# Byte offsets for split weights and gathered tokens, and 256-column gate/up matmuls in half of the experts

## The chip, the cores and the metric

One core of one Trainium2 chip. The metric is the device time of one execution in microseconds (us), the median of the runs shown. The inputs are fixed, so the tokens are routed in the same way in every run.

## The reference

Three transformer layers over 256 tokens of width 1024, in float32. Layer one mixes by bidirectional gated linear attention and windowed attention and has a dense SwiGLU of width 2816. Layers two and three mix by compressed attention and a gated recurrence; the second has a dense SwiGLU, the third a mixture of 8 experts of width 3584, of which each token takes two. The part that the change is about:

```python
logits = jnp.einsum('td,de->te', xf, w_router)
top_logits, top_idx = lax.top_k(logits, TOP_K)
gates = jax.nn.softmax(top_logits, axis=-1)
...
hid = jax.nn.silu(lax.ragged_dot(xs, w_gate, group_sizes)) * lax.ragged_dot(xs, w_up, group_sizes)
ys = lax.ragged_dot(hid, w_down, group_sizes)
```

## The kernel before

**Split weights.** Each product of float32 operands is made of three matmuls in the type `float32r`: both operands are split into a rounded part `hi` and a rest `lo`, and hi·hi, lo·hi and hi·lo are added up in PSUM. A weight arrives by SP's DMA as a `raw` tile of 128 partitions and up to 2048 floats (`load`, L148). `part_of` splits it in parts of 1024 floats: ScalarE copies it to `hi` (L160), VectorE subtracts (L161). The `hi` and `lo` tiles of a part come from a pool `hip` with three buffers of each, used in turn; until the mixture of experts begins, a fourth place in the turn is the pool `hip2` with one of each.

**Dense part (0 to about 930 us).** Most projections go through `feat`, whose matmuls are issued by the helper `mm` (L196): the weight's 128 columns are stationary, and 256 tokens move (256 columns). A part of 512 output features is 24 such matmuls, 16 with `hi` and 8 with `lo`. `ffn` issues its down projection through `mm` as well. Some projections go through `tok_part` (L225, L226, L228), with tokens stationary and 512 columns of the weight moving.

**Mixture of experts (about 945 us to the end).** `dispatch` gathers the tokens of a pair of experts into `xs` (hi and lo, 128 slots for each expert) by matmuls with one-hot maps (L1293). `expert` walks over 7 blocks of 512 hidden features. `up` computes gate and up: `xs` is stationary, 512 columns of the weight move, six matmuls to a part (L1371, L1372, L1374). `down` does the down projection (L1411, L1413, L1415), also with 512 moving columns; `turned` transposes the hidden block for it (L1392). An explicit order (`Steps`, under a manual schedule) lets the splitting run two parts ahead of the matmuls. Weights arrive in 14 `raw` buffers, used in the order `RAW_ORDER`; nine of them (`raw2`) lie over memory that the dense part's tiles give back, and the order of the list is that in which these bytes come free.

**Where the tiles lie.** In the program's allocation the start addresses in a partition, modulo 128 bytes, are:

| tile | bytes modulo 128 |
|---|---|
| `hi`, `lo` in `hip` (three of each) | 64 |
| `hi`, `lo` in `hip2` | 0 |
| dense activations `nh`, `nl`, `oh`, `ol`, attention's `hh`, `hl` and so on (pool `t4p`, 4096 bytes each) | 0 |
| gathered tokens `xs` (both) | 32 |
| hidden activations `th`, `tl` | 96 |
| dispatch: one-hot maps `oh` (moving), tokens `hh`, `hl` (stationary) | 32, 64 |

Steps of k and of columns inside these tiles are multiples of 512 bytes, so the table holds for every full-width matmul on them.

Of the kernel before, what the change touches and what calls it, by code (L numbers as in the profile page):

```python
# [10 lines left out]
F32 = mybir.dt.float32  # L11
# [8 lines left out]
P = 128  # L20
T = 256
NT = 2
# [11 lines left out]
# weight parts by which pieces of the arithmetic are put off, so that their operands are ready  # L34
# [4 lines left out]
RAW_BUFS, RAW2_BUFS, HI_BUFS, T4_BUFS, OHT_BUFS = 4, 9, 3, 16, 2  # L39

# [72 lines left out]
def tile_kernel(ctx: ExitStack, tc: tile.TileContext, a: dict, out: bass.AP, dbg=None, upto=99):  # L113
# [10 lines left out]
    hip = ctx.enter_context(tc.tile_pool(name="hip", bufs=HI_BUFS))  # L124
# [10 lines left out]
    hi_pools = [hip] * HI_BUFS  # L135
# [3 lines left out]
    # ---------------------------------------------------------------- weights  # L139
    def load(src, k0, kt, c, n, pieces=None):  # L140
        """Rows of k tiles k0.. and columns c.. of a weight; pieces: (column, width) in order."""
# [11 lines left out]
    def part_of(raw, k0, j, m, n):  # L153
        """k tiles j to j + m - 1 of a loaded weight, split in two."""
        pool = hi_pools[hi_turn[0] % len(hi_pools)]
        hi_turn[0] += 1
        hi = pool.tile([P, 1024], F32R, tag="hi", name="hi")[:, :m * n]
        rj = raw[:, j * n:(j + m) * n]
        lo = pool.tile([P, 1024], F32R, tag="lo", name="lo")[:, :m * n]
        nc.scalar.copy(hi, rj)  # L160
        lo_engine[0].tensor_sub(lo, rj, hi.bitcast(F32))  # L161
        return k0 + j, m, hi.rearrange("p (k n) -> p k n", n=n), lo.rearrange("p (k n) -> p k n", n=n)
# [3 lines left out]
    def unit(src, k0, kt, c, n, pieces=None):  # L166
        """A loaded weight's parts."""
# [9 lines left out]
    def defer(n, f):  # L177
        """f() after n more weight parts, and after what was deferred before."""
        queue.append((max([ticks[0] + n] + [d for d, _ in queue]), f))

    def run():
        """What is due."""
        while queue and queue[0][0] <= ticks[0]:
            queue.pop(0)[1]()
# [5 lines left out]
    def tick():  # L190
        """A weight part is done with."""
        ticks[0] += 1
        run()
# [4 lines left out]
    def feat(ps, x, src, c, widths, K, step=4, in_turn=False):  # L198
        """ps[:w, f, :] = src[:, c + f..].T @ x for feature blocks f (weights stationary); in_turn: block
        by block, so that the first are done early."""  # L200
# [18 lines left out]
    def tok_part(o, x, t, part, first, last, cs=slice(None)):  # L219
        """o += x.T @ part for one token tile."""  # L220
# [16 lines left out]
    # ---------------------------------------------------------------- small helpers  # L237
    def rsqrt_of(v, n, y=None):
        """v ** -0.5 on [P, n]."""
# [5 lines left out]
    def rsqrt(ss, n, dim):  # L245
        """(ss / dim + eps) ** -0.5 on [P, n]."""
# [9 lines left out]
    # ---- columns of vectors: gains of the norms ahead of the dense layers  # L256
# [31 lines left out]
    def squares(j, t):  # L288
        """Sum of squares over D of the half j of x, tokens on partitions."""
# [3 lines left out]
    def rstd(dst):  # L293
        """The factor of x's norm, tokens on partitions, from the sums of squares."""
# [6 lines left out]
    with ExitStack() as dense:  # L301
# [21 lines left out]
        class HL:  # L323
            """k-tiled operand kept in several tiles of four k each."""
# [8 lines left out]
        class Norm:  # L333
            """x times the gains n, feature-major and split; what is left of the norm is a factor per token:
            rt [P, t] with tokens on partitions, rb [P, T] along the free axis."""
# [10 lines left out]
            def block(self, k):  # L346
                """Feature block k of x is final."""
# [5 lines left out]
            def squares(self, j):  # L353
                """Blocks 4 j to 4 j + 3 are final."""
# [18 lines left out]
        def bcast_free(dst, cols_):  # L373
            """dst [P, T] = the token-major columns [P, t] along the free axis, on every partition."""
# [7 lines left out]
        def residual(ps, j, nt):  # L382
            """x's feature blocks 4 j to 4 j + 3 take ps [P, 4, T]; the norm nt takes them on."""
# [7 lines left out]
        def ffn(nt, w_gate, w_up, cg, cu, w_down, nxt):  # L391
            """x += (silu(h @ w_gate) * (h @ w_up)) @ w_down."""
# [4 lines left out]
            def down(b):  # L397
                f0, w, hh, hl = b
                for u0 in range(0, w // P, 2):
# [3 lines left out]
                    # feature block by feature block at the end, so that the first are done early  # L403
# [38 lines left out]
        # ============================================================ block 1  # L442
        with ExitStack() as b1:
# [37 lines left out]
            # columns of vectors: gate biases, rope gains  # L481
# [30 lines left out]
            # ---- GLA gates  # L512
# [25 lines left out]
            # ---- SWA projections  # L538
# [16 lines left out]
            def rope(z, nh, n):  # L555
                """z [P, nh, T] feature-major, in place."""
# [18 lines left out]
            for d in range(2):  # L575
# [5 lines left out]
                # factor across the two blocks: exp(r0 - tot0 - r1)  # L581
# [24 lines left out]
            # A[s, t] per head  # L606
# [3 lines left out]
            def scores(b):  # L610
# [5 lines left out]
                # block b of s against the other block of t: forward from 0 to 1, backward from 1 to 0  # L616
# [7 lines left out]
            # ---- SWA attention, by groups of four heads that share keys and values  # L624
# [102 lines left out]
            # ---- silu(r) * gain  # L727
# [10 lines left out]
            # ---- GLA output  # L738
# [37 lines left out]
            # ---- gates and the two output projections  # L776
            def gated(base, j, src, w):
                """sigmoid(h @ w_in[base..]) * (src @ w) for feature blocks 4 j to 4 j + 3."""
# [34 lines left out]
        # ============================================================ block 2  # L813
        b2p = dense.enter_context(tc.tile_pool(name="b2p", bufs=1))
        b2r = dense.enter_context(tc.tile_pool(name="b2r", bufs=1))
        # x itself is a buffer too until its tokens come back to the partitions
# [13 lines left out]
        # ---- rotary tables of the positions, [feature, token]  # L830
# [25 lines left out]
        # ---- columns of vectors  # L856
# [8 lines left out]
        # the second layer's lower bounds, from the cumulative softmax over the layers less its first row, and  # L865
        # what they leave of 1; the first layer's are that row less itself
# [21 lines left out]
        def hsplit(hi, lo, src, ncols_k, gcol):  # L888
            """hi + lo = src * gain, per k tile (gain varies over partitions and k)."""
# [6 lines left out]
        def layer_mix(l, nt, nxt):  # L896
            w_in = a["w_in_2"][l]
            hT, rt_, rb = nt.xT, nt.rt, nt.rb
            # ---- HGRN2: forget gates, keys (feature-major)
# [13 lines left out]
            # log of max(f, 1e-30) in two ranges, as Ln holds down to 2 ** -64  # L913
# [10 lines left out]
            # ---- HGRN2 queries  # L924
# [7 lines left out]
            # ---- HGRN2 attention matrix, from decays between tokens by binary splits  # L932
# [4 lines left out]
            def put(m, h, lhs, rhs):  # L937
                """A[s, t] for the pairs of level m: t in the right halves of 2 h tokens (all tokens if h is 0)."""
# [43 lines left out]
            # ---- MLA: compressed projections  # L982
# [16 lines left out]
            # rstd of both, token-major  # L999
# [23 lines left out]
            # k_pe, rotated, on both halves of the partitions  # L1023
# [12 lines left out]
            # queries  # L1036
# [26 lines left out]
            # keys and values  # L1063
# [23 lines left out]
            # ---- MLA attention  # L1087
# [44 lines left out]
            # ---- chunks of 64: from the chunk's start, and to its end  # L1132
# [29 lines left out]
            # ---- HGRN2 values, silu(g) * gain  # L1162
# [12 lines left out]
            # ---- HGRN2 output  # L1175
# [32 lines left out]
            for j in range(2):  # L1208
# [6 lines left out]
                # x, and the router's logits, short of the norm's factor  # L1215
                for i in range(4):
# [7 lines left out]
                    if k % 2:  # L1224
                        # x with tokens on partitions, and split for the dispatch
# [25 lines left out]
    # ================================================================ mixture of experts  # L1251
    with ExitStack() as moe:
# [6 lines left out]
        # in the order in which their bytes are left  # L1259
# [16 lines left out]
        def dispatch(base, pos_of, gate_of, n):  # L1276
            """One-hot maps and split inputs of n experts, for ranks base..base + 127, step by step."""
# [6 lines left out]
            xs = [m2.tile([P, KD, n * P], F32R, tag="xs%d" % i, name="xs", bufs=1) for i in range(2)]  # L1284
# [18 lines left out]
            # slot-major: who sits where, with which gate and factor  # L1303
# [370 lines left out]
```

## Time and profile before

| | |
|---|---|
| median of 3 runs | 1959.42 us (1956.49 to 1961.25) |
| profiled execution, first to last instruction (span) | 1958.2 us |
| TensorE (PE) busy | 1920.8 us, 98% |
| TensorE weight load (PEld) busy | 1686.8 us, 86% |
| VectorE (DVE) busy | 1534.9 us, 78% |
| ScalarE (ACT) busy | 1262.5 us, 64% |
| read from HBM | 501.20 MB, 256 GB/s over the span |

The profile gives no time of the profiled execution other than its span; the span is 1.2 us below the median, and inside the scatter of the runs. A matmul's record has a start that is measured and an end that is modelled, and records overlap; how fast matmuls follow each other is read from the starts, as the length of a stretch divided by the matmuls that start in it. A count in a row for a stretch contains those that began before it and are still under way. PEclk is the granted TensorE clock as a share of 2.4 GHz.

### The profile page before, as it was taken

Reading aid. Unit: us, or ns where it says so; the run is one execution under the profiler, and the core shown is the slowest. Engines: PE = TensorE matmul, PEld = TensorE weight load, DVE = VectorE, ACT = ScalarE, POOL = GpSimd, SP = SyncE. Lnnn points to the kernel's source line nnn. Section 1 sums busy time; section 2 is a strip of 40 time slices with the busy share of each in tenths; the row PEclk is TensorE's granted clock in tenths of the full one; section 3 lists DMA queues with packets and bytes.
Section 4 is the critical chain, followed back from the end, with each engine's and each line's share of the span. In section 5 each row is a group of like instructions: output and inputs, shape, how many; then the busy total and the mean of one; then the engine's idle time right before and its main releaser. Section 6 shows DMA issues by size and latency. Waiting matters only on the chain.

```text
span 1958.2 us, 29578 instructions
## 1 busy us (share of the span) xinstructions
PE 1920.8 (98%) x11581; PEld 1686.8 (86%) x11581; DVE 1534.9 (78%) x1648; ACT 1262.5 (64%) x1528; POOL 114.3 (6%) x111
## 2 busy tenths in 40 slices
PE   8999999999999999999899999999999999999997
PEld 7879999999989999988788888888888888888886
DVE  5865577557767555875788999889899898988997
ACT  5565455445665444655677777777777777777775
POOL 0110000000210000022000000000000000000000
PEclk9999999999999999999899999999999999999999
DMA  7435555554435555425899998999989999899990
GB/s 284 163 104 183 196 190 184 195 184 144 148 129 172 195 184 169 159 90 178 314 364 353 362 356 319 368 363 351 366 316 357 357 360 365 314 365 362 352 348 34
DMA packets 229458, 504.23 MB, mean 257 GB/s; under 512 B 12500, under 2 KB 25632, under 8 KB 229312
## 3 DMA queue, kind: packets, MB, share of 16 engines
q1 hardware_dynamic: 229312, 502.28, 72.0%
q8 instruction: 92, 1.51, 0.3%
q14 instruction: 54, 0.44, 0.1%
HBM read 501.20 MB, written 1.05 MB: 256 GB/s over the span
## 4 chain that ended last, share of the span: by engine, by line
PE 53%; DVE 1%; ACT 0%; POOL 0%; issue 0%; DVEq 0%; POOLq 0%; ACTq 0%
PE gu L1371 11%; PE gu L1372 11%; PE gu L1374 11%; PE pd L1411 5%; PE pd L1413 5%; PE pd L1415 5%; PE tp L1392 1%; PE tp L1293 1%; PE accum L196 1%; PE tp L1465 0%; PE tp L1466 0%; PE pa L1220 0%; PE tp L1307 0%; DVE hn L1613 0%; PE pd L1424 0%; PE pd L1428 0%
## 5 line engine op out<-in xcount | busy, mean ns | idle before, releaser
L161 DVE TENSOR_TENSOR lo<-raw,hi 128x1024 fp32r<-128x1024 f32 x937 | 1114.7, 1226 | 249.2 <-ACT hi L160 237.0
L160 ACT CAST hi<-raw 128x1024 fp32r<-128x1024 f32 x939 | 954.9, 1042 | 413.6 <-PE accum L196 213.9
L1371 PE MATMUL gu<-hi,xs 128*128 128x512 f32 x896 | 356.1, 397 | 0.0
L1372 PE MATMUL gu<-hi,xs 128*128 128x512 f32 x896 | 355.7, 397 | 0.0
L196 PE MATMUL accum<-nh,hi 128*128 128x256 f32 (+1 forms) x1192 | 288.0, 282 | 0.9 <-DVE hq L929 0.8
L196 PE MATMUL accum<-nl,hi 128*128 128x256 f32 (+1 forms) x1192 | 287.2, 281 | 0.4 <-DVE nl L351 0.4
L1374 PE MATMUL gu<-lo,xs 128*128 128x512 f32 x896 | 282.7, 397 | 0.0
L196 PEld LDWEIGHTS accum<-nh,hi 128*128 128x128 f32 (+1 forms) x1192 | 227.0, 190 | 2.2 <-ACT hi L160 0.9
L196 PEld LDWEIGHTS accum<-nl,hi 128*128 128x128 f32 (+1 forms) x1192 | 226.7, 190 | 1.1 <-DVE nl L351 0.7
L1374 PEld LDWEIGHTS gu<-lo,xs 128*128 128x128 f32 x896 | 168.9, 189 | 41.3
L1371 PEld LDWEIGHTS gu<-hi,xs 128*128 128x128 f32 x896 | 169.1, 189 | 40.7
L1372 PEld LDWEIGHTS gu<-hi,xs 128*128 128x128 f32 x896 | 169.0, 189 | 40.8
L196 PE MATMUL accum<-nh,lo 128*128 128x256 f32 (+1 forms) x1192 | 166.6, 281 | 2.4 <-DVE lo L161 2.4
L196 PEld LDWEIGHTS accum<-nh,lo 128*128 128x128 f32 (+1 forms) x1192 | 150.7, 190 | 3.5 <-DVE lo L161 2.8
L1411 PE MATMUL pd<-hi,th 128*128 128x512 f32 x440 | 143.0, 406 | 0.0
L1413 PE MATMUL pd<-hi,tl 128*128 128x512 f32 x440 | 138.4, 396 | 0.0
L1415 PE MATMUL pd<-lo,th 128*128 128x512 f32 x440 | 138.1, 395 | 0.0
L1415 PEld LDWEIGHTS pd<-lo,th 128*128 128x128 f32 x440 | 82.7, 188 | 20.2
L1413 PEld LDWEIGHTS pd<-hi,tl 128*128 128x128 f32 x440 | 82.6, 188 | 20.2
L196 PE MATMUL pa<-hh,lo 128*128 128x256 f32 x352 | 97.7, 278 | 0.0
L196 PE MATMUL pa<-hl,hi 128*128 128x256 f32 x352 | 97.7, 278 | 0.0
L196 PE MATMUL pa<-hh,hi 128*128 128x256 f32 x352 | 97.7, 278 | 0.0
(439 smaller groups left out, 2362.0 us busy)
## 6 DMA issues: line engine op xcount, KB each, us to landing
raw<-in_moe_w_gate_dram SPq DMA_DIRECT2D x112, 1024.0 KB
raw<-in_moe_w_up_dram SPq DMA_DIRECT2D x112, 1024.0 KB
raw<-in_moe_w_down_dram SPq DMA_DIRECT2D x112, 1024.0 KB
raw<-in_w_in_dram SPq DMA_DIRECT2D x40, 1024.0 KB
raw<-in_w_ffn_in_dram SPq DMA_DIRECT2D x22, 1024.0 KB
raw<-in_w_ffn_out_dram SPq DMA_DIRECT2D x11, 1024.0 KB
raw<-in_w_out_dram SPq DMA_DIRECT2D x10, 1024.0 KB
raw<-in_dense_w_up_dram SPq DMA_DIRECT2D x10, 1024.0 KB
```

What stands on the lines that cost most here:

```text
L160: nc.scalar.copy(hi, rj)
L161: lo_engine[0].tensor_sub(lo, rj, hi.bitcast(F32))
L196: nc.tensor.matmul(o, w, v, start=start, stop=stop, skip_group_check=True)
L1293: nc.tensor.matmul(px[:, kk, :n * P], src[:, t, (k + kk) * P:(k + kk + 1) * P], oh[:, t].rearrange("p n s -> p (n s)"), start=i == 0, stop ...
L1371: nc.tensor.matmul(st[key], xh[:, k, ss], hi[:, k - k0, :], start=k == 0, stop=False)
L1372: nc.tensor.matmul(st[key], xl[:, k, ss], hi[:, k - k0, :], start=False, stop=False)
L1374: nc.tensor.matmul(st[key], xh[:, k, ss], lo[:, k - k0, :], start=False, stop=k == KD - 1)
L1392: nc.tensor.transpose(pt[:, k * P:(k + 1) * P], hd[:, k * P:(k + 1) * P], ident)
L1411: nc.tensor.matmul(pd[z], th[:, ks], hi[:, 0, halves[z]], start=k == 0, stop=False)
L1413: nc.tensor.matmul(pd[z], tl[:, ks], hi[:, 0, halves[z]], start=False, stop=False)
L1415: nc.tensor.matmul(pd[z], th[:, ks], lo[:, 0, halves[z]], start=False, stop=k == 4 * nb - 1)
```

## The change

- `hip` becomes three pools of one buffer for each of `hi` and `lo`, with tiles of 1056 floats in place of 1024, and so do `hip2`'s. Within its tile a part's `hi` starts at the first and its `lo` at the second number of `SKEW` (in floats of 4 bytes). The turn through the pools is now counted from the start of the kernel, modulo the pools there are (four, later three).
- `xs` is allocated with 32 floats more, and its two tiles start at the offsets of `XSKEW`, one pair of offsets for each pair of experts.
- In experts 4 to 7, gate and up use two matmuls of 256 columns (the two halves of the PSUM bank) for each one of 512, with the same stationary operand. All gate/up matmuls are now issued through `mm`.
- Comments are deleted, and a tile `mm` is renamed `mx2`.

```diff
+SKEW = ((0, 4), (8, 12), (2, 20), (8, 12))
+XSKEW = ((0, 4), (8, 12), (16, 20), (24, 28))
+NARROW = (False, False, True, True)
+SPARE = 32
...
-    hip = ctx.enter_context(tc.tile_pool(name="hip", bufs=HI_BUFS))
+    hips = [ctx.enter_context(tc.tile_pool(name="hip%d" % n, bufs=1)) for n in range(HI_BUFS)]
...
-    hi_pools = [hip] * HI_BUFS
+    hi_pools = list(hips)
...
         pool = hi_pools[hi_turn[0] % len(hi_pools)]
+        at = SKEW[hi_turn[0] % len(hi_pools)]
         hi_turn[0] += 1
-        hi = pool.tile([P, 1024], F32R, tag="hi", name="hi")[:, :m * n]
+        hi = pool.tile([P, 1024 + SPARE], F32R, tag="hi", name="hi")[:, at[0]:at[0] + m * n]
         rj = raw[:, j * n:(j + m) * n]
-        lo = pool.tile([P, 1024], F32R, tag="lo", name="lo")[:, :m * n]
+        lo = pool.tile([P, 1024 + SPARE], F32R, tag="lo", name="lo")[:, at[1]:at[1] + m * n]
...
-            xs = [m2.tile([P, KD, n * P], F32R, tag="xs%d" % i, name="xs", bufs=1) for i in range(2)]
+            xs = []
+            for i in range(2):
+                z = m2.tile([P, KD * 2 * P + SPARE], F32R, tag="xs%d" % i, name="xs", bufs=1)
+                o = XSKEW[turn][i]
+                xs.append(z[:, o:o + KD * n * P].rearrange("p (k s) -> p k s", s=n * P))
...
+                    cols = [slice(0, 256), slice(256, 512)] if narrow else [slice(0, 512)]
                     for k in range(k0, k0 + m):
-                        nc.tensor.matmul(st[key], xh[:, k, ss], hi[:, k - k0, :], start=k == 0, stop=False)
-                        nc.tensor.matmul(st[key], xl[:, k, ss], hi[:, k - k0, :], start=False, stop=False)
+                        for z, w in ((xh, hi), (xl, hi)):
+                            for cs in cols:
+                                mm(st[key][:, cs], z[:, k, ss], w[:, k - k0, cs],
+                                   z is xh and k == 0 and cs.start == 0, False)
                     for k in range(k0, k0 + m):
-                        nc.tensor.matmul(st[key], xh[:, k, ss], lo[:, k - k0, :], start=False, stop=k == KD - 1)
+                        for cs in cols:
+                            mm(st[key][:, cs], xh[:, k, ss], lo[:, k - k0, cs], False, k == KD - 1)
...
-                              wg[e], wu[e], wd[e], hold)
+                              wg[e], wu[e], wd[e], hold, NARROW[e // 2])
```

The new tiles are 4224 bytes, 33 times 128, so every pool's start keeps its place modulo 128 bytes; tiles behind them move up by 768 or 1024 bytes. The start addresses after the change, modulo 128: `hi` and `lo` are at 64 and 80, at 96 and 112, at 72 and 16 in the three pools, and at 32 and 48 in `hip2`; `xs` (hi and lo) is at 32 and 48 for experts 0 and 1, at 64 and 80 for 2 and 3, at 96 and 112 for 4 and 5, at 0 and 16 for 6 and 7.

## Rows read from the trace of the kernel before

**Rows 1.** The page: busy time, and the chain that ended last by line

```profile
PE 1920.8 (98%) x11581; PEld 1686.8 (86%) x11581; DVE 1534.9 (78%) x1648; ACT 1262.5 (64%) x1528; POOL 114.3 (6%) x111
PE gu L1371 11%; PE gu L1372 11%; PE gu L1374 11%; PE pd L1411 5%; PE pd L1413 5%; PE pd L1415 5%; PE tp L1392 1%; PE tp L1293 1%; PE accum L196 1%; PE tp L1465 0%; PE tp L1466 0%; PE pa L1220 0%; PE tp L1307 0%; DVE hn L1613 0%; PE pd L1424 0%; PE pd L1428 0%
```

**Rows 2.** Stretches of 100 us: busy time by engine (instructions), clock, DMA share, GB/s

```profile
core 0: us, PE busy (x) PEld busy (x) DVE busy (x) ACT busy (x) POOL busy (x), PEclk, DMA share, GB/s
200.00:300.00 100.00, 99.42 (x860) 98.96 (x859) 67.06 (x65) 49.35 (x53) 3.94 (x2) 1.00 0.55 189
700.00:800.00 100.00, 100.00 (x872) 100.00 (x871) 62.90 (x59) 48.09 (x53) 6.36 (x3) 1.00 0.51 167
1200.00:1300.00 100.00, 100.00 (x442) 80.66 (x441) 90.50 (x87) 76.34 (x82) 0.00 (x0) 1.00 0.97 356
1500.00:1600.00 100.00, 100.00 (x442) 80.67 (x441) 90.15 (x86) 76.03 (x82) 0.00 (x0) 1.00 0.98 359
```

**Rows 3.** Stretches of L196's matmuls, one part of 24 each

```profile
215.77:218.49 2.72, 2.72 (x27) 2.72 (x26) 1.00 0.60 190
218.49:221.37 2.88, 2.88 (x27) 2.88 (x26) 1.00 0.52 198
221.37:224.09 2.72, 2.72 (x27) 2.72 (x26) 1.00 0.94 332
...
226.81:229.53 2.72, 2.72 (x27) 2.72 (x26) 1.00 0.55 160
229.53:232.41 2.88, 2.88 (x27) 2.88 (x26) 1.00 0.69 228
...
596.58:599.41 2.83, 2.83 (x27) 2.83 (x25) 1.00 0.00 0
```

**Rows 4.** Stretches of 512-column matmuls: six, six and 36 start in them

```profile
155.12:156.48 1.36, 1.36 (x8) 1.13 (x7) 0.61 (x1) 0.30 (x1) 0.00 (x0) 1.00 0.00 0
156.48:157.88 1.40, 1.40 (x8) 1.12 (x7) 0.62 (x1) 0.75 (x1) 0.00 (x0) 1.00 0.47 118
1066.41:1074.84 8.43, 8.43 (x37) 6.78 (x36) 7.00 (x7) 6.67 (x8) 0.00 (x0) 1.00 1.00 359
```

**Rows 5.** The chain in order of time, 1188 us: dispatch's 256-column matmuls

```profile
1188.52 0.95 PE tp L1293 x8
```

**Rows 6.** Groups of instructions by line and shape: count, busy us, mean ns

```profile
L1371 PE MATMUL gu<-hi,xs 128*128 128x512 f32 x896 | 356.1, 397 | 0.0
L196 PE MATMUL accum<-nh,hi 128*128 128x256 f32 x1176 | 284.3, 282 | 0.9 <-DVE hq L929 0.8 <-ACT nh L350 0.2
L196 PE MATMUL pa<-hh,hi 128*128 128x256 f32 x352 | 97.7, 278 | 0.0
L196 PE MATMUL accum<-oh,hi 128*128 128x256 f32 x128 | 33.3, 284 | 0.0
L196 PE MATMUL accum<-gol,hi 128*128 128x256 f32 x64 | 15.1, 278 | 0.0
L1411 PE MATMUL pd<-hi,th 128*128 128x512 f32 x440 | 143.0, 406 | 0.0
```

**Rows 7.** The splits at L161 from 1000 to 1900 us: duration ns min/median/max

```profile
L161 DVE TENSOR_TENSOR lo<-raw,hi x606: 1207/1219/1227, 999.5 to 1899.8; 128x1024 fp32r<-128x1024 f32 x152
```

**Rows 8.** In order of time around the experts' start: SP, ACT, POOL and PE

```profile
896.33 0.37 SPq L148 DMA_DIRECT2D raw<-in_moe_w_gate_dram  x1
931.41 3.39 SPq L148 DMA_DIRECT2D raw<-in_moe_w_up_dram  x2
919.42 2.00 ACT L160 CAST hi<-raw 128x1024 fp32r<-128x1024 f32 x2 [1.68 <-PE accum L196]
921.50 2.95 POOL L161 TENSOR_TENSOR lo<-raw,hi 128x1024 fp32r<-128x1024 f32 x1 [11.49 <-ACT hi L160]
954.65 2.93 ACT L160 CAST hi<-raw 128x1024 fp32r<-128x1024 f32 x3
944.07 0.63 PE L1371 MATMUL gu<-hi,xs 128*128 128x512 f32 x1
```

More of the change, by code (lines that the diff above doesn't have):

```diff
@@ L1274, in bc, with dispatch @@
             return z[:, :, None].to_broadcast([P, NT, NE])
-        def dispatch(base, pos_of, gate_of, n):
+        def dispatch(base, pos_of, gate_of, n, turn=0):
             oh = m2.tile([P, NT, n, P], F32R, tag="oh", name="oh", bufs=1)
@@ L1356, in run, with expert @@
                     self.now += 1
-        def expert(steps, xs, ss, ohT, gs, wg, wu, wd, hold=None):
+        def expert(steps, xs, ss, ohT, gs, wg, wu, wd, hold=None, narrow=False):
             nb = EXPERT_FF // 512
@@ L1491, in pair @@
         def pair(e0):
-            return dispatch(0, lambda t, j: pos[:, t, e0 + j:e0 + j + 1], lambda t, j: gr[:, t, e0 + j, :], 2)
+            return dispatch(0, lambda t, j: pos[:, t, e0 + j:e0 + j + 1], lambda t, j: gr[:, t, e0 + j, :], 2, e0 // 2)
         def dispatched(gen, box, steps):
@@ L1567, in tile_kernel @@
             nc.vector.tensor_scalar(one[n], place, float(n), None, op0=ALU.is_equal)
-        mm = mp.tile([P, 2, NT], F32, name="mm")
+        mx2 = mp.tile([P, 2, NT], F32, name="mx2")
         gp = mp.tile([P, 2, NT], F32, name="gp")
-        nc.vector.reduce_max(mm[:, 0, :], lg, axis=AX.X)
+        nc.vector.reduce_max(mx2[:, 0, :], lg, axis=AX.X)
         nc.vector.scalar_tensor_tensor(place, one[0], -3e38, lg, op0=ALU.mult, op1=ALU.add)
-        nc.vector.reduce_max(mm[:, 1, :], place, axis=AX.X)
-        nc.vector.tensor_sub(gp[:, 1, :], mm[:, 1, :], mm[:, 0, :])
+        nc.vector.reduce_max(mx2[:, 1, :], place, axis=AX.X)
+        nc.vector.tensor_sub(gp[:, 1, :], mx2[:, 1, :], mx2[:, 0, :])
         nc.vector.tensor_mul(gp[:, 1, :], gp[:, 1, :], rr)
```

## The prediction

> **What bounds the kernel now.** I read the page first, then stretches of 100 us, then the stretches of single parts. TensorE is busy for 98% of the span, and its gate, up and down matmuls hold half of the chain that ended last [rows 1]. The stretches show two regimes: 860 to 872 matmuls in 100 us in the dense part and 442 among the experts, with TensorE busy all of both, at the full clock of 2.4 GHz; among the experts DVE is busy for 90% and the DMA engines for 97% [rows 2]. So in most of the span the end is set by how closely matmuls follow each other, and the change can only act through that, or by making something else late.
>
> A matmul of 256 columns streams for 256/2.4 = 106.7 ns. In the dense part 24 of them take 2.72 us or 2.88 us, 113.3 or 120.0 ns each [rows 3]. The pattern repeats with every fourth part: three at the low level, one at the high. The turn has four places, and by the table of addresses three of these hold the weight 64 bytes off the tokens (modulo 128), the fourth, `hip2`, 0 bytes off. I take it that the fourth place is the slow one, since its address is what sets it apart. A stretch near 597 us has the good placement and still takes 2.83 us, 117.9 ns [rows 3], so the address is not all. The 512-column matmuls, 213.3 ns of streaming, take 226.7 or 233.3 ns with the weight 64 bytes off, and 36 in 8.43 us, 234.2 ns, among the experts, where it is 32 off [rows 4]. Two matmuls of 256 columns at the low level take 226.7 ns and at the high level 240.0, so one pair lies on either side of one wide matmul.
>
> **The dense part.** By the counts of a third of its 256-column matmuls [rows 6] there are 3 x (1176 + 352 + 128 + 64 + 64 + 64) = 5544, the two groups of 64 not shown being of the same kind, or 58 sets of four parts of 24. A set costs 72 x 113.3 + 24 x 120.0 = 11.04 us now. Afterwards only the 16 matmuls with the first pool's `hi` keep their place against the tokens. The other 80 lie 16 to 112 bytes off, in no case 0, and at none of these does the trace show a dense matmul. Bounds: all at the low level saves 24 x 6.7 x 58 = 9.3 us; all 80 at the high level costs 56 x 6.7 x 58 = 21.7 us. I take the middle, 116.7 ns, which is near the only 256-column row with another offset (dispatch's one-hot maps against tokens, 32 bytes off: eight in 0.95 us, 118.8 ns each [rows 5]): 16 x 113.3 + 80 x 116.7 = 11.15 us a set, **+6.4 us**.
>
> **Experts 4 to 7, gate and up.** Half of 3 x 896 = 2688 wide matmuls [rows 6] become 1344 pairs. The low level gives 7.5 ns back a pair, -10.1 us; the high level costs 5.8, +7.8 us. For experts 4 and 5 the offsets between weights and `xs` are 0, 16, 24 bytes and the like, and I take dispatch's 118.8 ns, from the same stage: 672 x (237.5 - 234.2) = +2.2 us. For experts 6 and 7 the first pool's `hi` is 64 bytes off the high half of `xs`, as in the good dense row; I take the middle, 233.4 ns a pair, -0.5 us. Together **+1.7 us**. Every half needs its own weight load; the dense part shows loads keeping up with matmuls 113.3 ns apart (PEld busy 100% [rows 2]), so the load is no new bound below that.
>
> **Experts 0 to 3, and the down projection.** 1344 wide matmuls of gate and up and 3 x 440 + 24 of down [rows 6] get new offsets. Wide matmuls 64 and 32 bytes off differ by about 1 ns [rows 4], so I take **0**. Bounds: all at the shortest, 226.7 ns, -20 us; all at twice the high level, +15 us. The DMA engines cap a gain: at 97% busy [rows 2] they leave about 3% of 1000 us, 30 us.
>
> **What costs nothing.** The renamed tile and the comments do nothing. DVE's split takes 1207 to 1227 ns whatever buffers it reads [rows 7]; were it slowed by an 8-byte start, its 10% of idle time among the experts would cover a tenth. Single-buffer pools rotate as the three did, except once: the first expert part takes the place of the last dense part instead of the next one. Its cast, now the second of the two at 919.42, must then wait for TensorE's last dense matmul near 931; the cast of 1 us and POOL's 2.95 us end by 935, and the first expert matmul is at 944.07 [rows 8]. Queued behind that cast on ACT are the copies of x for dispatch, which have the same cover.
>
> The larger tiles also move the dense activations up by 1024 bytes and the `raw2` buffers laid over them by 768, so that a `raw2` buffer reaches 256 bytes into one more dense tile. The fifth expert load, issued on SP at 896.33, then needs the tile that holds `ol` until the last dense matmuls, and SP's queue, which is in order, would hold it and all loads behind it until 931, where the thirteenth is issued now [rows 8]. ACT first wants the fifth in the last of the three casts from 954.65 [rows 8]; 1 MB at 356 GB/s [rows 2] takes 2.9 us. Cover: 20 us. **0**.
>
> **Sum.** 6.4 + 1.7 = +8.1 us on the span of 1958.2; the median of the runs is 1.2 us above the span, so 1967.5 us, 0.4% slower. A difference of 0.3%, 5.9 us, is about what a measurement can tell from none.
>
> **The rivals.** *The offsets end the stalls.* It is on the other side. If only 0 bytes off is bad, the dense part loses its fourth slow part (-9.3 us), and pairs at the low level save up to 10.1 us: 1940 us. For it: the one slow place is the one with 0 bytes off [rows 3]. Against: dispatch's 118.8 ns at 32 bytes off [rows 5], and 117.9 ns at 64 [rows 3]. It decides from a dense mean below 115.0 ns, the mean of 3 x 113.3 and 120.0. Chance 0.20.
>
> *The place is nothing.* If the fourth place is slow for another reason than its address, the dense part stays as it is and a pair takes twice the dense mean, 230.0 ns: 1344 x -4.2 = -5.6 us, 1954 us. Against it: nothing but the address sets the fourth place apart, and a reason tied to the place in the turn would have to spare the next three. Chance 0.25. The Trainium skill, "SBUF — State Buffer", section "Who interferes with whom", gives TensorE two independent read ports, for the moving operand and for the weight load, and says that it never waits on anyone; by that rule the place could do nothing. The trace does not bear it out: the same matmul takes 113.3 or 120.0 ns by its buffer [rows 3]. Its page "TensorE: Matmul & The Clock Gate", section "Wait — 56ns, not 53.3ns?", speaks against the narrow pairs: a stream of matmuls pays some 2.5 ns a matmul above its columns, by which 1344 more would cost an estimated 3.4 us; the trace's 6.7 and 20.9 ns above the columns [rows 3, 4] are not one such price.
>
> *The experts start late.* If the held loads or the cast cost more than their cover, TensorE stands still near 944; ten us past the cover gives 1977. Against it are 9 and 20 us of cover [rows 8]. Chance 0.05.
>
> **Chances and range.** The forecast has 0.50. Of it 0.10 lies within 0.3% (dense nearer the low level). The place being nothing sits on the edge of 0.3%, so 0.06 of its 0.25 counts as faster. Faster 0.20 + 0.06 = 0.26, same 0.10 + 0.19 = 0.29, slower 0.40 + 0.05 = 0.45. The range goes from 1944 (half of the first rival is below) to 1984 (the dense part's upper bound is 1959.4 + 21.7 = 1981, and the pairs add to it). The forecast's own range is 1961 to 1981.
>
> **What would show it.** Parts of 24 in the dense part: the first place mostly at 2.72 us, the others at 2.8 us instead of 2.72, and the fourth below 2.88. Pairs among experts 4 and 5 near 237 ns, and lower in 6 and 7; wide matmuls of experts 0 to 3 still near 234. The first expert matmul within 1 us of where it is now, measured from the last dense one. I am wrong if the fourth place alone changes, if wide matmuls move by more than 2 ns, or if TensorE idles near 944.

## The result, and the profile after

| | before | after |
|---|---|---|
| median, in one job | 1957.95 us | 1970.77 us (1969.29 to 1971.33) |
| span of the profiled execution | 1958.2 us | 1967.4 us |
| last matmul of the dense part starts | 930.88 us | 941.98 us (+11.10) |
| first expert matmul starts | 944.07 us | 955.49 us (+11.42) |
| from there to the end | 1014.11 us | 1011.91 us (-2.20) |

The kernel became slower: the ratio is 1.0061, with an interval of 1.0048 to 1.0075. One disturbed execution of 3842.47 us is left out. The forecast of 1967.5 us was right in sign and 3.3 us low, but the table shows that the sum was not put together as forecast: the dense part lost more than the whole, and the experts gave some of it back.

The page of the changed kernel, busy time and the chain by line, answers to [rows 1]. L202 is `mm`, L196 before; gate and up are now issued there too, which is why their three lines of before are one.

```profile
PE 1931.0 (98%) x12925; PEld 1764.6 (90%) x12925; DVE 1536.9 (78%) x1648; ACT 1262.7 (64%) x1528; POOL 115.6 (6%) x111
PE gu L202 32%; PE pd L1425 5%; PE pd L1427 5%; PE pd L1429 5%; PE tp L1406 1%; PE tp L1303 1%; PE accum L202 1%; PE tp L1479 0%; PE tp L1480 0%; PE tp L1317 0%; DVE hn L1627 0%; DVE ranks L1535 0%; PE pd L1438 0%; PE pd L1439 0%; PE pd L14
```

TensorE has 1344 matmuls more and is still busy for 98%; VectorE and ScalarE are as busy as they were. What bounds the kernel has not changed. The same stretches of 100 us as in [rows 2], for the changed kernel:

```profile
core 0: us, PE busy (x) PEld busy (x) DVE busy (x) ACT busy (x) POOL busy (x), PEclk, DMA share, GB/s
200.00:300.00 100.00, 99.52 (x839) 99.09 (x838) 64.69 (x65) 48.44 (x53) 1.95 (x2) 1.00 0.55 188
700.00:800.00 100.00, 100.00 (x846) 100.00 (x845) 56.28 (x51) 43.32 (x45) 6.33 (x3) 1.00 0.53 171
1200.00:1300.00 100.00, 100.00 (x450) 81.53 (x449) 91.33 (x89) 77.24 (x84) 0.00 (x0) 1.00 0.96 348
1500.00:1600.00 100.00, 100.00 (x714) 93.66 (x713) 89.28 (x85) 76.66 (x83) 0.00 (x0) 1.00 0.99 357
```

Busy time says nothing here: TensorE is 100% busy in both kernels, at the same granted clock. Read the counts. In the dense part 872 matmuls in 100 us became 846, so each takes longer; among experts 2 and 3 (1200 us) 442 became 450, so each takes less. The stretch at 1500 us has two narrow matmuls in place of each wide one of gate and up and can't be compared by its count.

Parts of 24 matmuls in the dense part, at L202 of the changed kernel (compare [rows 3]; start to start of a part, and its length):

```profile
212.95:215.79 2.84, 2.84 (x27) 2.84 (x25) 1.00 0.07 25
215.79:218.62 2.83, 2.83 (x27) 2.83 (x25) 1.00 0.62 201
218.62:221.46 2.84, 2.84 (x27) 2.84 (x25) 1.00 0.49 185
221.46:224.29 2.83, 2.83 (x26) 2.83 (x25) 1.00 0.88 334
```

The pattern of three parts at 2.72 us and one at 2.88 is gone. All four places take 2.83 or 2.84 us, 118.1 ns a matmul. Among the experts, parts of six 512-column matmuls of gate and up (experts 0 and 1), and of twelve 256-column ones (experts 4 and 5), both of the changed kernel:

```profile
1060.06:1061.46 1.40, 1.40 (x8) 1.14 (x6) 1.00 1.04 402
1061.46:1062.84 1.38, 1.38 (x7) 1.13 (x6) 1.00 1.06 405
1062.84:1064.23 1.39, 1.39 (x7) 1.12 (x6) 1.00 1.07 396
...
1643.72:1645.14 1.42, 1.42 (x12) 1.42 (x12) 1.00 1.06 405
1645.14:1646.56 1.42, 1.42 (x15) 1.42 (x14) 1.00 0.81 251
```

A wide part was 8.43/6 = 1.405 us before [rows 4] and is about 1.39 now; a part that became narrow takes 1.42. And the start of the experts, TensorE in order of time, changed kernel:

```profile
941.86 0.40 PE L202 MATMUL accum<-oh,lo 128*128 128x256 f32 x2
942.77 0.61 PE L1226 MATMUL pa<-wr,xT 128*128 128x8 f32 x4 [0.51 <-DVE xT L1224]
...
949.73 0.35 PE L1564 MATMUL tp<-sel,ranks 128*128 128x8 f32 x1 [3.84 <-DVE one L1581]
...
955.49 0.89 PE L202 MATMUL gu<-hi,xs 128*128 128x512 f32 x3
```

What TensorE waits for here is the routing on VectorE, in both kernels (3.70 us before, 3.84 now at the longest). No weight and no cast is late.

### The profile page after: what moved, and what is told of

It reads as the page before. It is cut to its first block, busy times and chain, and to the rows that moved or that the text cites. A ratio compares the mean times of both kernels' runs of the same rounds, so it can differ in the third digit from the quotient of the medians.

```text
span 1967.4 us, 32281 instructions
## 1 busy us (share of the span) xinstructions
PE 1931.0 (98%) x12925; PEld 1764.6 (90%) x12925; DVE 1536.9 (78%) x1648; ACT 1262.7 (64%) x1528; POOL 115.6 (6%) x111
## 4 chain that ended last, share of the span: by engine, by line
PE 52%; DVE 1%; ACT 0%; POOL 0%; issue 0%; DVEq 0%; POOLq 0%; ACTq 0%
PE gu L202 32%; PE pd L1425 5%; PE pd L1427 5%; PE pd L1429 5%; PE tp L1406 1%; PE tp L1303 1%; PE accum L202 1%; PE tp L1479 0%; PE tp L1480 0%; PE tp L1317 0%; DVE hn L1627 0%; DVE ranks L1535 0%; PE pd L1438 0%; PE pd L1439 0%; PE pd L1442 0%; DVE x L1452 0%
## 5 line engine op out<-in xcount | busy, mean ns | idle before, releaser
L202 PE MATMUL gu<-hi,xs 128*128 128x256 f32 (+1 forms) x2688 | 493.2, 319 | 0.0
L202 PEld LDWEIGHTS gu<-hi,xs 128*128 128x128 f32 x2688 | 398.8, 189 | 41.3
L202 PE MATMUL accum<-nh,hi 128*128 128x256 f32 (+1 forms) x1192 | 292.4, 284 | 0.8 <-DVE hq L935 0.5
L202 PE MATMUL accum<-nl,hi 128*128 128x256 f32 (+1 forms) x1192 | 292.0, 282 | 0.6 <-DVE nl L357 0.6
L202 PE MATMUL gu<-lo,xs 128*128 128x256 f32 (+1 forms) x1344 | 282.9, 319 | 0.0
L202 PEld LDWEIGHTS accum<-nh,hi 128*128 128x128 f32 (+1 forms) x1192 | 225.6, 189 | 1.9 <-ACT hi L166 0.7
L202 PEld LDWEIGHTS accum<-nl,hi 128*128 128x128 f32 (+1 forms) x1192 | 224.8, 189 | 1.5 <-DVE nl L357 0.8
L202 PEld LDWEIGHTS gu<-lo,xs 128*128 128x128 f32 x1344 | 206.3, 189 | 19.5
L202 PE MATMUL accum<-nh,lo 128*128 128x256 f32 (+1 forms) x1192 | 169.5, 284 | 0.0
L202 PEld LDWEIGHTS accum<-nh,lo 128*128 128x128 f32 (+1 forms) x1192 | 153.5, 189 | 1.0 <-issue 0.7
L202 PE MATMUL pa<-hh,lo 128*128 128x256 f32 x352 | 99.0, 281 | 0.0
L202 PE MATMUL pa<-hl,hi 128*128 128x256 f32 x352 | 98.8, 281 | 0.0
L202 PE MATMUL pa<-hh,hi 128*128 128x256 f32 x352 | 98.8, 281 | 0.0
L1425 PEld LDWEIGHTS pd<-hi,th 128*128 128x128 f32 x440 | 76.2, 189 | 11.1
L259 ACT CAST th<-tp 128x512 fp32r<-128x512 f32 x56 | 32.9, 587 | 69.2 <-PE tp L1406 69.2
```

Source lines behind the costliest of these rows:

```text
L202: nc.tensor.matmul(o, w, v, start=start, stop=stop, skip_group_check=True)
L259: nc.scalar.copy(hi, src)
L1425: nc.tensor.matmul(pd[z], th[:, ks], hi[:, 0, halves[z]], start=k == 0, stop=False)
```

## The experiments

All twelve are the changed kernel with other values of `SKEW` (one pair of offsets, hi and lo in floats, for each place in the turn), `XSKEW` (the same for `xs`, one pair for each pair of experts) and `NARROW`; the last one needs a second pair for the experts as well. In the diffs the new values are shown, those they replace are the change's. Their results, with before and after, stand in this table. The pitches are means of start to start over recorded matmuls that follow each other without a wait: dense is all 256-column matmuls after 224 us, wide and narrow are gate and up with 512 and 256 columns. Stretches in which the granted clock was at half speed are not in these means.

| run | ratio to before, interval | dense ns | first expert matmul us | wide ns | narrow ns | experts to the end us |
|---|---|---|---|---|---|---|
| before | 1 | 115.6 | 944.1 | 234.3 | | 1014.1 |
| after | 1.0061 [1.0048, 1.0075] | 118.4 | 955.5 | 231.9 | 118.6 | 1011.9 |
| e1 | 0.9995 [0.9986, 1.0004] | 116.0 | 945.8 | 231.1 | 117.5 | 1010.1 |
| e2 | 1.0075 [1.0061, 1.0088] | 118.4 | 957.2 | 232.0 | 118.9 | 1012.6 |
| e3 | 1.0031 [1.0020, 1.0042] | 118.4 | 957.3 | 231.7 | | 1005.5 |
| e9 | 0.9964 [0.9950, 0.9978] | 116.0 | 941.7 | 230.1 | | 1002.3 |
| e4 | 0.9892 [0.9876, 0.9908] | 113.6 | 933.4 | 230.1 | | 1003.9 |
| e7 | 0.9995 [0.9986, 1.0004] | 117.1 | 949.3 | 232.1 | | 1005.4 |
| e10 | 1.0078 [1.0064, 1.0092] | 119.1 | 959.5 | | 116.7 | 1011.6 |
| e5 | 0.9918 [0.9904, 0.9931] | 113.6 | 933.5 | 231.9 | | 1007.4 |
| e11 | 0.9920 [0.9907, 0.9934] | 113.6 | 932.4 | 232.6 | | 1009.3 |
| e6 | 0.9962 [0.9948, 0.9975] | 113.6 | 932.4 | | 117.7 | 1015.7 |
| e8 | 0.9963 [0.9950, 0.9977] | 113.6 | 932.6 | | 117.7 | 1016.3 |
| e12 | 0.9967 [0.9955, 0.9979] | 113.6 | 933.4 | | 117.7 | 1016.3 |

**e1: the weights back at the start of their tiles.**

```
-SKEW = ((0, 4), (8, 12), (2, 20), (8, 12))
+SKEW = ((0, 0), (0, 0), (0, 0), (0, 0))
```

> The changed kernel with every offset of the split weights set to 0; its pools, larger tiles, token offsets and narrow matmuls stay. Theory O (the offset between weight and tokens sets how closely the dense matmuls follow): parts of 24 go back to 2.72, 2.72, 2.72 and 2.88 us, the first expert matmul comes at 943 to 946 us instead of 955, and the time is 1957 to 1963 us. Theory P (the pools of one buffer, the turn counted anew and the moved tiles cost the time): parts stay at 2.83 us or TensorE waits more, and the time stays at 1968 to 1973 us.

Parts of 24 at L202 in this run:

```profile
214.45:217.17 2.72, 2.72 (x27) 2.72 (x26) 1.00 0.17 63
217.17:219.89 2.72, 2.72 (x27) 2.72 (x25) 1.00 0.64 176
219.89:222.75 2.86, 2.86 (x27) 2.86 (x25) 1.00 0.59 222
222.75:225.54 2.79, 2.79 (x27) 2.79 (x25) 1.00 0.84 313
```

The levels of before are back, 2.72 and nearly 2.88 us, and with them 1957.34 us, 13.4 less than after. The weights' offsets made the dense part slower; theory P, by which the pools of one buffer, the turn or the moved tiles cost the time, falls. One thing differs from before: the part that follows the slow one takes 2.79 us, though it stands 64 off, where before it took 2.72. In this part the 16 matmuls with `hi` take 117.9 ns each and the 8 with `lo` 113.4.

**e2: the tokens' offsets taken back, e3: all experts wide.** Each undoes one part of the change and leaves the other two.

```
e2: -XSKEW = ((0, 4), (8, 12), (16, 20), (24, 28))
    +XSKEW = ((0, 0), (0, 0), (0, 0), (0, 0))
e3: -NARROW = (False, False, True, True)
    +NARROW = (False, False, False, False)
```

> The changed kernel with all gathered tokens at offset 0 (32 bytes past a multiple of 128 for every pair of experts). Theory O: the dense part is that of the changed kernel (first expert matmul near 955 us); the wide matmuls of experts 0 to 3 move from 231.9 ns back towards 233, the pairs of experts 4 to 7 stay at 236 to 238 ns; the time is 1970 to 1975 us. Rival: the token offsets are what slows the experts 4 to 7, and the pairs drop to 230 ns, 1962 us.

> The changed kernel with 512-column matmuls in all experts. Theory O: only experts 4 to 7 change, from 237.1 ns a pair to about 232 ns a wide matmul, 1344 x -5 = -7 us, so 1962 to 1966 us, still slower than before by the dense part. Rival N (the narrow matmuls are the main cost): the time falls to that of before, 1958 us, or below.

The tokens' places alone change nothing that can be told: wide 232.0 instead of 231.9 ns, narrow 118.9 instead of 118.6, 1971.97 us. The narrow matmuls cost 7.1 us (1970.77 - 1963.70), and the pitch accounts for it: 1344 pairs by 2 x 118.6 - 231.7 = 5.5 ns are 7.4 us.

**e9: only the larger tiles.** No offset and no narrow matmul; what is left of the change is the pools of one buffer and the 128 bytes more in each tile. Together they put each `lo` and the lower half of `xs` an odd number of times 128 bytes behind its `hi`, where it was a multiple of 256.

```
+SKEW = ((0, 0), (0, 0), (0, 0), (0, 0))
+XSKEW = ((0, 0), (0, 0), (0, 0), (0, 0))
+NARROW = (False, False, False, False)
```

> All offsets 0 and wide matmuls everywhere: against the kernel before only the pools of one buffer and the larger tiles are left, by which lo and the low half of the tokens lie an odd multiple of 128 bytes behind the high ones instead of a multiple of 256. Theory S (this alone shortens the experts' wide matmuls): dense parts 2.72, 2.72, 2.72, 2.88 us as before, wide matmuls near 230 ns instead of 234, time 1945 to 1950 us. Rival (the wide matmuls got shorter in e4 by the fourth place's offset or the shorter dense part): wide matmuls at 234 ns, time 1956 to 1960 us.

Two wide parts of six matmuls, one behind the other, in this run:

```profile
1060.47:1061.85 1.38, 1.38 (x8) 1.13 (x7) 1.00 1.11 384
1061.85:1063.23 1.38, 1.38 (x8) 1.13 (x7) 1.00 0.94 352
```

1.38/6 = 230.0 ns, against 234.2 [rows 4]. So the gain on gate and up came from a side effect, the tiles' sizes and pools; the offsets took 1.8 ns of it back (231.9 in after). The down projection reads the same weight tiles and got nothing from it: by the same reckoning its wide matmuls take 233.5 ns before and 233.7 here. This run, at 1950.04 us, is faster than before: 0.9964 [0.9950, 0.9978].

**e4: the fourth place at 64, nothing else.** The larger tiles stay; `hip2`'s parts start 64 bytes into their tiles, so that all four places stand 64 bytes off the dense tokens.

```
-SKEW = ((0, 4), (8, 12), (2, 20), (8, 12))
+SKEW = ((0, 0), (0, 0), (0, 0), (16, 16))
+XSKEW = ((0, 0), (0, 0), (0, 0), (0, 0))
+NARROW = (False, False, False, False)
```

> All offsets 0 but the fourth place's, which is 64 bytes for hi and lo, so that all four places lie 64 bytes off the dense tokens; tokens of the experts as before, wide matmuls. Theory O: the parts of the fourth place go from 2.88 to 2.72 us like the other three, the dense part is 5 to 9 us shorter than before, the time 1949 to 1954 us. Rival Q (the fourth place is slow for another reason than its address, such as its place in the turn): it stays at 2.88 us and the time at 1957 to 1960 us.

Parts of 24 in this run:

```profile
215.33:218.05 2.72, 2.72 (x26) 2.72 (x25) 1.00 0.56 175
218.05:220.77 2.72, 2.72 (x26) 2.72 (x25) 1.00 0.61 221
220.77:223.49 2.72, 2.72 (x26) 2.72 (x25) 1.00 0.81 303
223.49:226.21 2.72, 2.72 (x26) 2.72 (x25) 1.00 0.20 78
```

Two stretches of 100 us of the same run, with the columns of [rows 2]:

```profile
200.00:300.00 100.00, 99.40 (x871) 98.95 (x870) 68.33 (x71) 50.39 (x54) 4.01 (x2) 1.00 0.58 190
1200.00:1300.00 100.00, 100.00 (x448) 81.46 (x447) 89.82 (x83) 78.05 (x84) 0.00 (x0) 1.00 1.00 363
```

All four places take 2.72 us. The last dense matmul is 11.07 us earlier than before, more than the 5 to 9 us expected, and the experts are 10.2 us shorter. At 1937.76 us this is the fastest kernel of the study, 0.9892 [0.9876, 0.9908] of before. It was expected nearer to before, because the shorter wide matmuls were not yet known: e9 showed where they came from. Not every part of this run is fast. Behind a wait of TensorE (1.32 us idle before 794.63 us), two parts with the good placement are slow, and only the third is back at 2.72:

```profile
796.08:798.91 2.83, 2.83 (x27) 2.83 (x25) 1.00 0.52 198
798.91:801.72 2.81, 2.81 (x27) 2.81 (x26) 1.00 0.03 9
801.72:804.44 2.72, 2.72 (x27) 2.72 (x26) 1.00 0.62 175
```

So the good placement lets a part run at 113.3 ns and doesn't ensure it: what went before counts too.

**e7: hi and lo of a part at the same offset.** The three pools stand 80, 96 and 112 bytes off the dense tokens, the fourth place 64.

```
+SKEW = ((4, 4), (8, 8), (12, 12), (16, 16))
+XSKEW = ((0, 0), (0, 0), (0, 0), (0, 0))
+NARROW = (False, False, False, False)
```

> The kernel of e9 with hi and lo of a place at the same offset: 80, 96, 112 and, in the fourth place, 64 bytes off the dense tokens. Theory O: parts in the first three places take 2.80 to 2.88 us, those in the fourth are the shortest, and the dense part is as long as the changed kernel's (first expert matmul 950 to 956 us), time 1958 to 1966 us. Rival X (the changed kernel lost because hi and lo of one part lay at different offsets): 2.72 us in all places, time as e4, 1936 to 1942 us.

Parts of 24 in this run; the second is the place at 64:

```profile
215.13:217.96 2.83, 2.83 (x26) 2.83 (x25) 1.00 0.62 200
217.96:220.70 2.74, 2.74 (x26) 2.74 (x25) 1.00 0.49 185
220.70:223.52 2.82, 2.82 (x27) 2.82 (x26) 1.00 0.90 324
223.52:226.34 2.82, 2.82 (x27) 2.82 (x25) 1.00 0.12 44
```

117.3 to 117.9 ns at 80, 96 and 112, 114.1 at 64. It isn't that the two halves of a part differ in their offset: they don't here, and the three parts are as slow as in the changed kernel. At these offsets, neither 0 nor 64, a matmul loses (117.6 - 113.3)/(119.2 - 113.3), some seven tenths, of what it loses at 0 (e10).

**e10: every dense place 0 bytes off.** All weights at 0 and `xs` at 64, so that among the experts the moving operand stands at 0 and the stationary one at 64, as in the fast dense rows (there the weight is the stationary one, here the moving one); all experts narrow.

```
+SKEW = ((16, 16), (16, 16), (16, 16), (0, 0))
+XSKEW = ((8, 8), (8, 8), (8, 8), (8, 8))
+NARROW = (True, True, True, True)
```

> All split weights at 0 bytes and the gathered tokens at 64 (modulo 128), narrow matmuls in all experts. In the dense part weight and tokens are then 0 bytes apart in all places: by theory O every part takes 2.88 us, and the dense part is 15 to 25 us longer than e4's. Among the experts the moving operand is at 0 and the stationary at 64, as in the good dense rows. Theory O2 (the two addresses themselves count, not which operand is the weight): 113.3 ns, 227 ns a pair, so that gate and up give back 2688 x -8 = -22 us against e6, time 1940 to 1955 us. Rival M (narrow matmuls among the experts are held near 118 ns by something other than these addresses): 235 ns a pair, time 1965 to 1975 us.

Parts of 24 in the dense part, and parts of twelve narrow matmuls among the experts:

```profile
213.68:216.54 2.86, 2.86 (x26) 2.86 (x25) 1.00 0.12 44
216.54:219.40 2.86, 2.86 (x26) 2.86 (x25) 1.00 0.61 186
...
1060.70:1062.09 1.39, 1.39 (x12) 1.39 (x12) 1.00 0.85 305
1062.09:1063.50 1.41, 1.41 (x14) 1.41 (x13) 1.00 1.04 399
```

All dense parts are slow, 2.86/24 = 119.2 ns, also in the three places that were fast in before. With e4 that makes the cause sure on both sides: the place in the turn does nothing, the weight's start does. The dense tokens stand at 0 modulo 128 in every run, so no run tells whether it is the weight's distance from them or the weight's own address that counts. Among the experts the narrow matmuls take 116.7 ns, less than in any other run, but far from 113.3.

**e5, e6, e8: the same dense part as e4, other tokens.** `xs` at 0 modulo 128 (64 off the weights) with wide matmuls (e5) and narrow ones (e6), and `xs` at 32 with narrow ones (e8).

```
+SKEW = ((0, 0), (0, 0), (0, 0), (16, 16))
e5, e6: +XSKEW = ((24, 24), (24, 24), (24, 24), (24, 24))
e8:     +XSKEW = ((0, 0), (0, 0), (0, 0), (0, 0))
e5:     +NARROW = (False, False, False, False)
e6, e8: +NARROW = (True, True, True, True)
```

> The kernel of e4 with the gathered tokens moved by 96 bytes, to a multiple of 128, so that weights lie 64 bytes off them as in the dense part. Theory O, if it holds for wide matmuls: 226.7 to 228 ns instead of 230.1, 2688 x -2 to -3.4 = -6 to -9 us, 1929 to 1932 us. Rival W (wide matmuls do not mind this offset): 1936 to 1939 us.

> The kernel of e5 with 256-column gate/up matmuls in all experts. Theory O: they run as the dense ones do 64 bytes off, 113.3 ns or 226.7 ns a pair, time 1928 to 1932 us. Rival M (narrow matmuls among the experts are held at about 118 ns by something other than the offset): 236 ns a pair, 2688 x 6 = +16 us on e4, 1952 to 1956 us.

> The kernel of e4 (tokens 32 bytes past a multiple of 128, weights 64) with 256-column gate/up matmuls in all experts. Theory O: 117 to 119 ns each, 236 ns a pair against 230.1, 2688 x 6 = +16 us, 1951 to 1956 us. Rival (narrow is as good as wide at any offset that is even over a whole part, and the changed kernel lost by mixing offsets): 227 to 231 ns a pair, 1928 to 1940 us.

The distance that goes with fast dense matmuls does nothing for the experts: wide 231.9 ns at 64 off against 230.1 at 32 off (e5, e4), narrow 117.7 ns at both (e6, e8). e8 is e4 with narrow matmuls and nothing else: the experts take 12.4 us more, and 2,688 more matmuls by 2 x 117.7 - 230.1 = 5.3 ns would be 14.2. By the rule of the Trainium skill, "TensorE: Matmul & The Clock Gate", section "Wait — 56ns, not 53.3ns?", the price of a further matmul is 2.5 ns; these runs have about twice that.

**e11: the tokens' lower half moved by another 128 bytes.** This takes back, for `xs` alone, what the larger tile did to the distance between the two halves.

```
+SKEW = ((0, 0), (0, 0), (0, 0), (16, 16))
+XSKEW = ((0, 32), (0, 32), (0, 32), (0, 32))
+NARROW = (False, False, False, False)
```

> The kernel of e4 with the low half of the gathered tokens 128 bytes further on, so that it lies again a multiple of 256 bytes behind the high half, as in the kernel before. If the tokens' two halves are what shortened the wide matmuls in e9: back to 234 ns, 2688 x 4 = +11 us on e4, 1946 to 1950 us. If the weights' two halves are: still 230 ns, 1936 to 1940 us. A value between says both.

Wide parts in this run:

```profile
1000.02:1001.43 1.41, 1.41 (x6) 1.13 (x6) 1.00 1.04 391
1001.43:1002.82 1.39, 1.39 (x8) 1.12 (x6) 1.00 1.07 370
```

The mean goes from 230.1 to 232.6 ns, with every second part or so back at 1.40 or 1.41 us. So moving the tokens' lower half by 128 bytes takes back 2.5 of the 4.2 ns that came with the larger tiles. That the distance between the halves is the reason isn't shown: e5 moves both halves by 96 bytes, leaves their distance as it is, and loses 1.8 ns. Whether the weights' halves gave the rest was not tried alone, and the down projection, which got nothing in e9, speaks against it.

**e12: the experts with the dense part's addresses modulo 256.** The moving operand at 0 and the stationary one at 192, as in the dense rows that take 113.3 ns. `SKEW_MOE` serves the experts, `SKEW` the dense part, and `wide` gives the widths of the `hi` and `lo` tiles.

```
+SKEW = ((0, 16), (0, 16), (0, 16), (16, 16))
+SKEW_MOE = (16, 0)
+XSKEW = ((40, 40), (40, 40), (40, 40), (40, 40))
+        at = SKEW[hi_turn[0] % 4] if len(hi_pools) == 4 else SKEW_MOE
+        wide = (1056, 1056) if len(hi_pools) == 4 and hi_turn[0] % 4 == 3 else (1040, 1072)
...
-                z = m2.tile([P, KD * 2 * P + SPARE], F32R, tag="xs%d" % i, name="xs", bufs=1)
+                z = m2.tile([P, KD * 2 * P + 64], F32R, tag="xs%d" % i, name="xs", bufs=1)
...
+NARROW = (True, True, True, True)
```

> The edit is made on the kernel with the tokens at 0 and 256-column matmuls in all experts (1949.96 us, 117.6 ns a matmul among the experts). Among the experts hi and lo of the weights move to 0, counted in bytes modulo 256, and both halves of the tokens to 192, so that moving and stationary operand stand there exactly as in the dense rows that take 113.3 ns. Theory A (the addresses modulo 256 are all that sets a 256-column matmul's pitch): 113.3 ns, 227 ns a pair; 2,688 pairs by 8.6 ns less is 23 us, so 1926 to 1930 us, or a little above where the weights' transfers set the pace. Rival M (something other than these addresses holds the 256-column matmul of the experts near 117 to 118 ns): 117 to 118 ns as before, 1946 to 1951 us. The dense part is the same in both: 113.3 ns, first expert matmul near 934 us.

Parts of twelve narrow matmuls in this run (their line is L204 here):

```profile
1001.87:1003.28 1.41, 1.41 (x14) 1.41 (x13) 1.00 1.05 394
1003.28:1004.69 1.41, 1.41 (x14) 1.41 (x13) 1.00 1.02 327
```

A stretch of 100 us of the same run:

```profile
1200.00:1300.00 100.00, 100.00 (x727) 94.00 (x726) 88.64 (x83) 76.68 (x82) 0.00 (x0) 1.00 0.99 362
```

117.7 ns, as in e6 and e8, and 1951.25 us. The start addresses modulo 256 are not all that sets the pitch; something in the experts' stage holds a 256-column matmul there. Two differences from the dense part are in the rows: VectorE is busy for 89% instead of 68, and the DMA engines for 99% instead of 58 (the row at 200 us of e4). But late in this run, when the weights have come, there is a part of twelve without any transfer and with VectorE busy for 44%:

```profile
1918.63:1920.04 1.41, 1.41 (x15) 1.41 (x13) 0.62 (x1) 1.21 (x2) 0.00 (x0) 1.00 0.00 0
```

It takes the same 1.41 us, so neither the transfers nor VectorE holds the pitch there. The order in which operands are used differs too: here two matmuls in a row have the same stationary operand. That was not tried by itself, so the cause stays open.

## Why the prediction was right in its sum, and where its terms were off

By its own signs of being wrong it failed in one: wide matmuls moved by 2.4 ns, more than the 2 it allowed. The fourth place did not change alone, and TensorE does not idle near the start of the experts more than before.

**What bounds the kernel: right.** TensorE is 100% busy in the stretches of before, after and e4 at the same clock, and most of the change in time is in how closely matmuls follow each other.

**Dense part: mechanism right, size too small.** The step that failed is "16 x 113.3 + 80 x 116.7": no place was left at 113.3, and the others were nearer 118. The first pool's `hi` kept its 64 bytes, yet its part, the one at 221.46 us of after, took 2.83 us, and the 16 matmuls with `hi` in it took 117.8 ns each. The forecast raised the mean by 1.1 ns and had +6.4 us; it rose from 115.6 to 118.4. Over some 4,880 matmuls after 224 us that is 2.8 x 4880 = 13.7 us, and between the same two matmuls the trace is 10.88 us longer (706.81 to 717.69 us). The other 3 us are the clock: in this part of the kernel the granted clock falls for a short time from 2.4 to 1.2 GHz, three times in before and once in after, each time behind pauses of TensorE. These are the 10 us around each fall, three of before and one of after:

```profile
480.00:490.00 10.00, 9.57 (x66) 9.55 (x67) 5.82 (x9) 6.16 (x7) 0.14 (x1) 0.83 0.43 131
517.00:527.00 10.00, 8.98 (x63) 8.84 (x64) 8.83 (x12) 4.90 (x8) 1.89 (x1) 0.83 0.01 2
840.00:850.00 10.00, 8.76 (x62) 8.38 (x61) 9.46 (x12) 5.40 (x9) 2.25 (x2) 0.83 0.01 2
...
520.00:530.00 10.00, 8.66 (x55) 7.89 (x54) 9.29 (x13) 5.59 (x10) 4.09 (x3) 0.83 0.00 0
```

Each row loses 0.17 of 10 us, some 1.7 us, and before has two more of them: an estimated 3.4 us that hid part of what the offsets cost. The upper bound of the step, "all 80 at the high level", was near what e10 measured, and the lower one, all at the low level, is e4. So the bounds were sound and the middle was not a good guess: e7's parts at the three offsets that lie between take 117.3 to 117.9 ns a matmul, on the side of the slow end. Dispatch's row [rows 5] with its 118.8 ns had been the nearer one to go by. Why matmuls at 64 bytes are slowed beside others is only suggested by e1 (2.79 us behind a slow part) and e7 (2.74 us between slow parts).

**Experts 0 to 3 and down: the step "differ by about 1 ns", from which the term was taken as 0, failed.** The rows that it rests on also hold a part at 226.7 ns, 7.5 below the experts' pitch [rows 4], so they did not show that placement is worth nothing. Wide gate and up went from 234.3 to 231.9 ns, and down from 233.5 to 231.9: 1344 x -2.4 - 1344 x 1.6 = -5.4 us. For gate and up the reason was in the change in plain sight, as tiles of 1056 floats, and the prediction took modulo 128 as the whole address, by which "every pool's start keeps its place". By e9 the larger tiles and their pools, which move the `lo` halves only if counted modulo 256, are worth 4.2 ns, and the offsets take 1.8 back. Down gained nothing in e9. It is at 231.8 to 232.2 ns in the four runs with weights at the change's offsets or e7's (after, e2, e3, e7) and at 232.2 to 233.9 in the others; why is open.

**Narrow pairs: right for experts 4 and 5, wrong for 6 and 7.** 118.5 and 118.6 ns were measured, 237.0 and 237.3 a pair, where 237.5 and 233.4 were forecast. The term is 1344 x (237.15 - 234.3) = +3.8 us instead of +1.7. The step that failed is that `hi` at 64 off would lower the pairs "as in the good dense row": e5, e6 and e12 show that the good row doesn't carry over to the experts.

**The start of the experts: right.** From the last dense matmul to the first of the experts it took 13.19 us before and takes 13.51, and no weight is waited for.

**The sum.** +11.1 to the last dense matmul, +0.3 at the start, -5.4 + 3.8 = -1.6 for the experts by the pitches (-2.2 measured): with the measured one 9.2 us on the span, against the 8.1 forecast. The dense part came out 4.7 us above its term and the experts 3.9 below theirs. That the two errors had opposite signs was luck, and so were the 3.4 us of clock, for which the prediction has no term: by the pitches alone the dense part would have lost 13.7. The profiled execution is also the fastest of its kernel; by the medians the loss is 12.8 us.

**The rivals.** That the place is nothing is ruled out by e4 and e10: 24 matmuls of the same shape take 2.72, 2.82 or 2.86 us by where their weights lie. The Trainium skill, "SBUF — State Buffer", section "Who interferes with whom", gives TensorE two independent read ports and says that it waits on no one. These times don't agree with what the prediction drew from it, that the place could do nothing; what makes the matmuls wait isn't shown. That the offsets end the stalls was wrong for the offsets of this change, since those in between are slow as well; but its core, that the fourth place costs 9.3 us in the dense part, was right in kind and somewhat low: e4, which differs from e9 in that place alone, is 12.3 us faster, and 116.0 - 113.6 = 2.4 ns on 4,880 matmuls are 11.7 us. (In the two traces the experts start only 8.4 us apart, because e4's dense part has two falls of the clock and e9's none.) That the experts start late didn't happen.

## What to carry to other kernels

When TensorE is 100% busy, count the matmuls in a stretch: pitches of 113.3 and 120 ns look alike in busy time. Here, with the dense tokens at 0, the start of the weights in bytes modulo 128 set it, with 64 the fast one of those tried and 0 the slowest. Try one value for all buffers rather than a spread of values, and look at what a tile's new size does to everything behind it: e4 keeps the larger tiles, sets one offset right, and takes 1.1% off.

## What was not expected of the hardware

- Dense 256-column matmuls on 128x128 weights, with tokens at 0 modulo 128, take 113.3 ns with all weights at 64 (e4), 117.3 to 117.9 at 80, 96 and 112 (e7) and 119.2 to 120.0 at 0 (e10, before), in the same stage, at the granted clock of 1.00.
- Matmuls at the good offset are slow in some parts: 117.8 ns with `hi` at 64 and `lo` at 80 in after, and for whole parts 116.4 behind a slow part in e1, 114.1 between slow parts in e7, 117.9 and 116.9 behind a wait in e4. The parts that stand where 117.9 was read at 596 us of before [rows 3] take 113.3 in e4. So a slow neighbour isn't needed; what starts and ends the slow state wasn't tested.
- For the 512-column matmuls of gate and up 128 bytes mattered: 234.3 ns before, 230.1 with 128 bytes more in the tiles, 232.6 with the tokens' lower half moved by another 128. For those of down the larger tiles did nothing (233.5 and 233.7).
- Among the experts no placement brought the mean of the 256-column matmuls below 116.7 ns, and they were no faster in a part without transfers (e12).
